# A hybrid decoder block with a product-key expert FFN: fewer dense key columns, other lists of experts gathered, and another order of the up lists

## The chip, the cores and the metric

The kernel runs on one core of one Trainium2 chip. The metric is the device time of one execution in microseconds (us), as the median of several executions. Beside the times there is one profiled execution with its trace; its times are those of single instructions on each engine.

## What is computed

One decoder layer on 256 tokens of width 2048, all in float32. An in-projection, stick-breaking attention and a chunked SSD scan, and an out-projection give h. Then comes the part that the change touches, a product-key expert layer (PEER):

```python
q = (xt @ w_query).reshape(t, 8, 2, 128)
scores = einsum('thcd,hckd->thck', q, sub_keys)          # 128 keys a half
top_s, top_i = top_k(scores, 16)
cand_i = top_i[:, :, 0, :, None] * 128 + top_i[:, :, 1, None, :]
best_s, best_pos = top_k(cand_s, 16)
expert_idx = take_along_axis(cand_i, best_pos)           # 16 of 16384 experts
gates = softmax(best_s)
act = gelu(einsum('thkd,td->thk', expert_down[expert_idx], xt))
out = einsum('thk,thkd->td', gates * act, expert_up[expert_idx])
```

So 256 tokens pick 8 x 16 experts each out of a grid of 128 x 128, and each expert has one row of 2048 numbers in the down table and one in the up table.

## The kernel before

**The front of the layer** is a stream of items (a load and the multiplications that use it), which TensorE (PE) works off in the order of the program. At its end stand 16 query items (name pq, line 253), each followed by the scores of its keys (sc, L896) and, on VectorE (DVE), by the choice of the best keys (MAX8 and FIND_INDEX8 at L900 and L901 and the reductions at L1004 to L1011).

**Dense columns.** For the last NDN columns of the key grid the product of all 128 experts with all 256 tokens is computed, whether a token picked them or not: dense(i), two items of eight float32 multiplications (dn<-xt_t,raw_dn, L253) on a load of 512 KB each, and a gelu that goes to a table in memory (zd_dram). FILL[hc] says how many of these columns stand behind query hc; all others stand behind the last query, as cover for the listing.

**The listing** (listing()) is a generator that the items advance. It transposes the picks (trT, L1115 and L1116), counts by which tokens each expert is used, ranks the experts and sorts them into NTS = 111 lists of 128 experts. yield from rest(n) lets n steps of other work pass. Before the first transposes stands rest(YT). A list's kind says who uses its experts: kinds 0 and 1 have experts that a single token of the first or second half of the tokens uses; kinds 2 and 3 have experts that two or more tokens of one half use; kinds 4 to 7 have those used in two quarters of different halves; kind 8 (C) is the rest. CAPS gives the lists of each kind. The first SPC lists of each kind hold experts from the other columns and are called sparse: their down rows are gathered by index (L1355, issued by GpSimd, POOL) and multiplied. The lists behind them hold experts of the dense columns: their values are fetched from zd_dram instead. The up rows of all lists are gathered.

**The units** multiply the down rows. unit_c(r) takes a C list: 4 items of 4 transposes (tc, L1523) and 12 multiplications of 128x256 (L1540 to L1542). unit_t(k, r) takes two lists of kinds 2 to 7: 8 items of 4 transposes (tp, L1465), a split into a high and a low part (ScalarE, ACT, at L1442 and DVE at L1443) and 6 multiplications (L1482 to L1484), and at the end two transposes back (z<-ident,zt, L1498), of which there is one pair per unit. unit_d takes a list of kind 0 or 1, a D unit: 4 items of 2 multiplications of 128x512 that give each row its token (xe or xt<-hnt,ot, L1609) and a sum over products on DVE (L1615). Beside the first units run the gates (gates(), groups g<-A,B at L1256). The units go C, then T; from the T unit with index DU = 7 on, D units are put between the items of the T units, DN of them in all.

**The up lists.** For each list 128 up rows of 2048 float32 (1.05 MB) come into a slot of a ring (5 slots during the units, 9 from begin() on). up_load splits the two halves of the row tile into a high part (ACT, L1827 or L1831) and a low part (DVE, L1828 or L1832; tile lo_up or x), and up_go multiplies both (out<-..., L1894, 128x512) with the list's weights p. split_p makes these weights: a split pair for most lists (12 multiplications for a list of one half, 24 for a C list), a one-hot matrix for sparse lists of kinds 0 and 1 (8 multiplications; the row's value is a scale of L1831 and L1832). Lists for which plain(n) holds are multiplied as they are, in float32: no split, no work on ACT or DVE for their rows, 4 multiplications.

**The order of the up lists** has an early part and three phases. The early lists are mixed with the last D units, by a time put beside each (timed); I call that the mixed stage. The early lists before are 29: two dense lists of kind 0 and the twelve lists of kind 2 (all split), then the fifteen sparse lists of kind 0, plain with a one-hot matrix scaled by the row's value (L1767). Phase 0 then has 46 lists (17 of kind 1, 12 of kind 3, 17 C), phases 1 and 2 have 18 each (14 lists of kinds 4 and 5, or 6 and 7, and NCX or NCY = 4 C lists). At the end of each phase the sums are moved (turn, L1868); the last ones are stored.

Of the kernel before, what the change touches and what calls it, by code (L numbers as in the profile page):

```python
# [14 lines left out]
OP = mybir.AluOpType  # L15
# [3 lines left out]
P = 128  # L19
T = 256  # L20
# [41 lines left out]
NCONST = K_LO + 2  # L62

NE = NK * NK
NDN = 20
NSC = NK - NDN
SPC = (15, 15, 10, 10, 6, 6, 6, 6, 20)
CAPS = (17, 17, 12, 12, 7, 7, 7, 7, 25)
LC = len(CAPS) - 1
BASE = [sum(CAPS[:k]) for k in range(LC + 1)]  # L70
# [19 lines left out]
ILAG = 2  # L90
YR = 2
YC = 2
YT = 2
GR = 1.0
KP = 0
GW = 3
# [1 line left out]
ZLAG = 4  # L98
OLAG = 7
TF = 10  # L100
XZ = 16
HU = 3
GU = 5
DU = 7
DN = 19
NPG = 4
YF = 3
HNP = 16
# [6 lines left out]
NA = 4  # L115
TD = -3
HY = 1
FILL = (0,) * 9 + (1, 0, 0, 1, 0, 0, 0)
PLP = 3
NCX = 4  # L120
NCY = 4
EV = 1
EF = (3, 1)
LP = 5
# [19 lines left out]
def tile_block(ctx: ExitStack, tc: tile.TileContext, xT, w_f, w_v, w_dt, w_o, w_q, sk, dnt, down, up,  # L144
# [55 lines left out]
    def wtile(shape, name, dt=F32):  # L200
        return wk.tile(shape, dt, tag="w", bufs=6, name=name)
# [1163 lines left out]
        pump()  # L1365

    def zh(n, w=P):
        if n < 8:
            return part["xa"][:, 3072 + P * n:3072 + P * n + w]
        if n < XZ:  # L1370
            return part["zr"][:, P * (n - 8):P * (n - 8) + w]
        n -= XZ
        if n == 0:
            gated(2)
        if n < 32:
            return held("zh", "b0")[:, P * n:P * n + w]
        return held("zh2", "b1")[:, P * (n - 32):P * (n - 32) + w]
# [6 lines left out]
    def zc(r):  # L1384
        if r < 16:
            return held("zc", "xb")[:, T * r:T * (r + 1)]
        return part["xa"][:, 2048 + T * (r - 16):2048 + T * (r - 15)]

    def zd(j):
        n = dn_of[j]  # L1390
        o = max(NTH - XZ - 32, 0) * P + sum(T if kind[i] == LC else P for i, m in dn_of.items() if m < n)
        return held("zh2", "b1")[:, o:o + (T if kind[j] == LC else P)]
# [20 lines left out]
    def dcol(k, n=1):  # L1413
        if "dsc" not in gens:
            gens["dsc"] = cp.tile([P, 8 * NDT + 128], F32, tag="gi", bufs=1, name="dsc")
        return gens["dsc"][:, NDT * k:NDT * (k + n)]
# [294 lines left out]
    for i, (_, k, r) in enumerate(ts_):  # L1711
        u_mark.append(len(items))
        u = unit_t(k, r)
        gathers += [("down", BASE[k] + r + x) for x in range(2)]
        more = 2 if len(left) > len(ts_) - i else 1
        for x in range(more if i >= DU else 0):
            n = left.pop(0)
            gathers.append(("down", d_list[n]))
            u[8 * x:8 * x + 4] = [v for p in zip(u[8 * x:8 * x + 4], dus[n]) for v in p]
        items.extend(u)  # L1720
# [3 lines left out]

    runs = [list(range(BASE[k], BASE[k] + CAPS[k])) for k in range(LC + 1)]
    ncs = (CAPS[LC] - NCX - NCY, NCX, NCY)
    order = [*runs[0][SPC[0]:], *runs[2][SPC[2]:], *runs[2][:SPC[2]], *runs[0][:SPC[0]]]
    early = len(order)
    phase = [0] * early
    for f in range(3):  # L1730
        c = runs[LC][sum(ncs[:f]):sum(ncs[:f + 1])]
        own = [runs[k] for k in range(LC) if PHASE[k] == f and k not in (0, 2)]
        if f < 2:
            order += [c[0], *mixed(*own, c[1:-1]), c[-1]]
        else:
            order += [c[0], *mixed(own[0], own[1][:-3], c[1:]), *own[1][-3:]]
        phase += [f] * (len(order) - len(phase))
# [15 lines left out]


    def plain(n):
        return n < early and kind[order[n]] == 0 and sparse[order[n]]

    def split_p(n):
        if n >= NTS or n in pw:
            return  # L1760
        j = order[n]
        k = kind[j]
        f = phase[n]
        if plain(n):
            ph = wtile([P, T], f"p{n}")[:, 0:P]
            d = d_of[j]
            TS(ph, iota[:, :, 0], dcol(7)[:, d:d + 1], dcol(2)[:, d:d + 1], op0=OP.is_equal, op1=OP.mult)  # L1767
            pw[n] = (ph, None)
            return
        if k < 2 and sparse[j]:  # L1770
            ph = wtile([P, T], f"p{n}", F32R)[:, 0:P]
            TS(ph, iota[:, :, 0], dcol(7)[:, d_of[j]:d_of[j] + 1], None, op0=OP.is_equal)
            pw[n] = (ph, None)
            return
        while j not in multiplied:
            work()
        src = zd(j) if not sparse[j] else zh(th_of[j]) if k < LC else zc(j - BASE[LC])
        if k < LC:
            w2 = wtile([P, T], f"p{n}", F32R)
            ph, pl_ = w2[:, 0:P], w2[:, P:T]  # L1780
        elif j % 2:
            ph, pl_ = [wtile([P, T], f"p{x}{n}", F32R) for x in "hl"]
        else:
            w2 = wide(f"p{n}", (P, 2 * T), F32R)
            ph, pl_ = w2[:, 0:T], w2[:, T:2 * T]
        if k < LC:
            cuts = [(slice(0, P), src[:, 0:P])]
        else:
            cuts = p_cuts(src, k, f)
        for sl, v in cuts:  # L1790
            h_, l_ = ph[:, sl], pl_[:, sl]
            if len(v.shape) == 3:
                h_, l_ = w3(h_, 64), w3(l_, 64)
            nc.scalar.activation(h_, v, AF.Copy)
            eng = nc.gpsimd if len(pw) % PLP == PLP - 1 and len(pw) > 8 else nc.vector
            eng.tensor_tensor(l_, v, h_.bitcast(F32), op=OP.subtract)
        pw[n] = (ph, pl_)
# [360 lines left out]
```

## Time and profile before

| | |
|---|---|
| Time, 3 runs | 1619.64 us median (1615.75 to 1621.01) |
| The profiled execution's own time | 1618.38 us |
| Its span, first to last instruction | 1616.5 us |
| Mean granted TensorE clock | 0.998 |
| PE busy | 1578.9 us, 98% of the span |
| DVE, ACT, POOL busy | 71%, 48%, 32% |

The span is what the views of the trace divide up; the execution's own time is 1.9 us longer. Shares of the span are means over stages that differ: a stage has to be read by itself, in a window of its own.

### The profile page before, as it was taken

How to read it: one execution, taken by the hardware profiler on the slowest of the kernel's cores; microseconds unless marked ns; L12 is line 12 of the kernel's file. 1: busy time of each engine (PE TensorE's matmuls, PEld its weight loads, DVE VectorE, ACT ScalarE, POOL GpSimd, SP SyncE). 2: the span in 40 equal slices, each digit the busy share in tenths (PEclk: the TensorE clock that was granted, in tenths of full speed). 3: DMA queues.
4: the chain of work that ended last, by engine and by line, in shares of the span. 5: the costliest groups of instructions: out<-in, count | busy, mean ns of one | idle time of the engine just before them, and what ended most of it. 6: DMA issues, size and time to landing. Idle time of an engine off the chain costs nothing.

```text
span 1616.5 us, 27319 instructions
## 1 busy us (share of the span) xinstructions
PE 1578.9 (98%) x10330; PEld 1403.3 (87%) x10331; DVE 1155.1 (71%) x2558; ACT 781.3 (48%) x1377; POOL 510.9 (32%) x495
## 2 busy tenths in 40 slices
PE   7999999999999999999999999999999999999997
PEld 7999978999888888889999999889986558887886
DVE  7776666864487988757637755878789347888896
ACT  7554557754111200525535566446555026667764
POOL 0001101111000000034415414555566455874650
PEclk9999999999999999999999999999999999999999
DMA  7555554667745534253393297788889998997983
GB/s 232 166 174 155 157 157 133 188 203 226 238 144 150 163 92 120 64 202 108 120 325 105 85 320 270 276 306 331 305 309 416 389 385 325 345 356 279 338 306 113
DMA packets 108808, 366.70 MB, mean 227 GB/s; under 512 B 12704, under 2 KB 48800, under 8 KB 82304
## 3 DMA queue, kind: packets, MB, share of 16 engines
q0 software_dynamic: 35504, 229.43, 38.3%
q1 hardware_dynamic: 70304, 134.23, 27.3%
q8 instruction: 83, 1.36, 0.3%
q10 hardware_dynamic: 2864, 1.24, 0.3%
q14 instruction: 53, 0.43, 0.1%
HBM read 337.24 MB, written 27.92 MB: 226 GB/s over the span
## 4 chain that ended last, share of the span: by engine, by line
PE 89%; DVE 5%; DMA 3%; issue 1%; ACT 1%; POOL 0%; SPq 0%; DVEq 0%; ACTq 0%; POOLq 0%
PE out L1894 21%; PE pq L253 7%; PE dn L253 7%; PE tp L1465 4%; PE g L1256 4%; PE v L735 3%; PE zc L1540 2%; PE zc L1541 2%; PE zc L1542 2%; PE z L1483 2%; PE tc L1523 2%; PE z L1484 2%; PE z L1482 2%; PE kq L312 2%; PE wo L318 2%; PE cnt L1057 2%
## 5 line engine op out<-in xcount | busy, mean ns | idle before, releaser
L1894 PE MATMUL out<-hi_up,p 128*128 128x512 f32 x716 | 193.2, 392 | 2.2 <-ACT hi_up L1827 2.2
L1894 PEld LDWEIGHTS out<-hi_up,p 128*128 128x128 f32 x716 | 134.0, 189 | 31.9 <-ACT hi_up L1827 3.9
L1443 DVE TENSOR_TENSOR t<-tp,t 128x512 fp32r<-128x512 f32 x176 | 119.7, 688 | 58.3 <-ACT t L1442 57.7
L253 PE MATMUL dn<-xt_t,raw_dn 128*128 128x256 f32 x640 | 158.6, 383 | 0.1
L1355 POOL DMA_INDIRECT raws<-in_down,idx x69 | 69.8, 1011 | 269.4 <-DVE colt L1196 161.9
L1442 ACT ACTIVATE t<-tp 128x512 fp32r<-128x512 f32 x176 | 102.8, 598 | 80.6 <-PE tp L1465 80.0
L1420 POOL DMA_INDIRECT raw_small<-g_dram,idx x111 | 119.8, 1080 | 42.5 <-issue 26.6
L253 PEld LDWEIGHTS dn<-xt_t,raw_dn 128*128 128x128 f32 x640 | 115.1, 193 | 11.6 <-issue 0.5
L253 PE MATMUL pq<-hg,raw_pq 128*128 128x256 f32 x512 | 112.9, 379 | 0.0
L253 PEld LDWEIGHTS pq<-hg,raw_pq 128*128 128x128 f32 x512 | 96.3, 190 | 12.5
L1259 ACT ACTIVATE big<-g 128x128 f32<-128x128 f32 x256 | 70.6, 436 | 74.0 <-PE g L1256 72.9
L1465 PE MATMUL tp<-ident,raws 128*128 128x128 f32 x624 | 100.4, 273 | 1.3 <-DMA raws<-in_down,idx 1.0
L1540 PE MATMUL zc<-hnl,c 128*128 128x256 f32 x320 | 96.0, 300 | 0.0
L1827 ACT ACTIVATE hi_up<-raws 128x1024 fp32r<-128x1024 f32 x74 | 77.2, 1058 | 36.7 <-PE out L1894 33.3
L1248 POOL TENSOR_TENSOR B<-B,gi 128x512 bf16<-128x512 bf16 x64 | 69.8, 1090 | 76.3 <-DVE B L1246 74.9
L1542 PE MATMUL zc<-hnl,c 128*128 128x256 f32 x320 | 89.1, 278 | 0.0
L1541 PE MATMUL zc<-hnl,c 128*128 128x256 f32 x320 | 89.1, 278 | 0.0
L1443 DVE TENSOR_TENSOR c<-tc,c 128x512 fp32r<-128x512 f32 x80 | 55.1, 690 | 39.5 <-ACT c L1442 39.1
L1827 ACT ACTIVATE hi_up<-rows_hn 128x1024 fp32r<-128x1024 f32 x66 | 69.2, 1057 | 28.2 <-PE out L1894 23.6
L1249 DVE TENSOR_TENSOR A<-O,gi 128x1024 f16<-128x1024 bf16 x64 | 49.6, 775 | 41.7 <-PE g L1256 41.6
L1894 PE MATMUL out<-lo_up,p 128*128 128x512 f32 x254 | 76.9, 395 | 1.8 <-DVE lo_up L1828 1.8
L1355 POOL DMA_INDIRECT raws<-in_up,idx x49 | 60.8, 1241 | 53.7 <-DVE lo_up L1828 17.2
(538 smaller groups left out, 4591.0 us busy)
## 6 DMA issues: line engine op xcount, KB each, us to landing
raw_dn<-in_dnt SPq DMA_DIRECT2D x40, 512.0 KB, 3.8
raw_kq<-in_w_f SPq DMA_DIRECT2D x32, 512.0 KB, 3.8
raw_wo<-in_w_o SPq DMA_DIRECT2D x32, 512.0 KB, 4.5
raw_pq<-in_w_q SPq DMA_DIRECT2D x32, 512.0 KB, 3.8
g_dram<-big SPq DMA_DIRECT2D x16, 1024.0 KB, 16.3
raw_xb<-in_w_f SPq DMA_DIRECT2D x22, 512.0 KB, 4.5
raw_v<-in_w_v SPq DMA_DIRECT2D x16, 512.0 KB, 3.6
raw_z<-in_w_f SPq DMA_DIRECT2D x16, 512.0 KB, 3.8
```

The costliest lines, as they stand in the source:

```text
L253: nc.tensor.matmul(acc, raw[:, j * P:(j + 1) * P], mv[:, k * 8 + j, :], start=(k + j == 0), stop=(k * 8 + j == ND - 1))
L1259: nc.scalar.activation(gbuf[c][:, :, o:o + G2T].rearrange("p i t -> p t i"), gp[:, :, 32 * c:32 * c + 32], AF.Copy)
L1355: g = nc.gpsimd.indirect_dma_start(out=where[what, j], out_offset=None, in_=down_rows if what == "down" else up_rows, in_offset=bass.Indir ...
L1420: nc.gpsimd.indirect_dma_start(out=dst, out_offset=None, in_=g_half if w == P else g_dram, in_offset=bass.IndirectOffsetOnAxis(ap=idx[:, 1 ...
L1442: a = nc.scalar.activation(hi, tp, AF.Copy).ins
L1443: d = nc.vector.tensor_tensor(lo, tp, hi.bitcast(F32), op=OP.subtract).ins
L1465: nc.tensor.transpose(tp[:, (2 * dd + i) * P:(2 * dd + i + 1) * P], row("down", j + i)[:, d * P:(d + 1) * P], ident)
L1540: nc.tensor.matmul(z, wh, ah[:, d, :], start=(d == 0), stop=False)
L1541: nc.tensor.matmul(z, wh, al[:, d, :], start=False, stop=False)
L1542: nc.tensor.matmul(z, wl, ah[:, d, :], start=False, stop=(d == ND - 1))
L1827: marks["act"] = nc.scalar.activation(hi, raw, AF.Copy).ins
L1894: nc.tensor.matmul(oa[tt][2 * hf + c], w[:, k * P:(k + 1) * P], mv[:, c * 512:(c + 1) * 512], start=(i == starts[f, tt, hf] and mv is hi a ...
```

## The change

Four dense columns fewer (NDN 20 to 16), all of them now behind the last query (FILL). Two C lists more are sparse (SPC 20 to 22), so two lists fewer are fetched from zd_dram. YT goes from 2 to 9. Twenty-four D units instead of 19 stand in the T units, spread evenly: nine of the fifteen T units take two and six take one, where before the first four took two. The early lists are now 8 sparse lists of kind 2, and these are plain: the up rows are multiplied in float32 with the float32 weights (zh). The 17 lists of kind 0 and the 4 other lists of kind 2 go to phase 0, mixed with those of kinds 1 and 3, and are split there; the lists of kind 0 get the one-hot form of L1772. NCX and NCY go from 4 to 2, so phase 0 has 21 C lists and 71 lists in all, and phases 1 and 2 have 16 each. XZ and zh place the weights elsewhere.

```diff
--- before.py
+++ after.py
@@ -62,9 +62,9 @@
 NCONST = K_LO + 2
 
 NE = NK * NK
-NDN = 20
+NDN = 16
 NSC = NK - NDN
-SPC = (15, 15, 10, 10, 6, 6, 6, 6, 20)
+SPC = (15, 15, 10, 10, 6, 6, 6, 6, 22)
 CAPS = (17, 17, 12, 12, 7, 7, 7, 7, 25)
 LC = len(CAPS) - 1
 BASE = [sum(CAPS[:k]) for k in range(LC + 1)]
@@ -90,7 +90,7 @@
 ILAG = 2
 YR = 2
 YC = 2
-YT = 2
+YT = 9
 GR = 1.0
 KP = 0
 GW = 3
@@ -98,11 +98,12 @@
 ZLAG = 4
 OLAG = 7
 TF = 10
-XZ = 16
+XZ = 12
 HU = 3
 GU = 5
 DU = 7
-DN = 19
+DN = 24
+NE0 = 8
 NPG = 4
 YF = 3
 HNP = 16
@@ -115,10 +116,10 @@
 NA = 4
 TD = -3
 HY = 1
-FILL = (0,) * 9 + (1, 0, 0, 1, 0, 0, 0)
+FILL = (0,) * 16
 PLP = 3
-NCX = 4
-NCY = 4
+NCX = 2
+NCY = 2
 EV = 1
 EF = (3, 1)
 LP = 5
@@ -1365,10 +1366,10 @@
         pump()
 
     def zh(n, w=P):
-        if n < 8:
-            return part["xa"][:, 3072 + P * n:3072 + P * n + w]
+        if n < 4:
+            return part["xa"][:, 3584 + P * n:3584 + P * n + w]
         if n < XZ:
-            return part["zr"][:, P * (n - 8):P * (n - 8) + w]
+            return part["zr"][:, P * (n - 4):P * (n - 4) + w]
         n -= XZ
         if n == 0:
             gated(2)
@@ -1712,7 +1713,7 @@
         u_mark.append(len(items))
         u = unit_t(k, r)
         gathers += [("down", BASE[k] + r + x) for x in range(2)]
-        more = 2 if len(left) > len(ts_) - i else 1
+        more = 2 if (i - DU) * (DN - len(ts_) + DU) % (len(ts_) - DU) < DN - len(ts_) + DU else 1
         for x in range(more if i >= DU else 0):
             n = left.pop(0)
             gathers.append(("down", d_list[n]))
@@ -1724,12 +1725,12 @@
 
     runs = [list(range(BASE[k], BASE[k] + CAPS[k])) for k in range(LC + 1)]
     ncs = (CAPS[LC] - NCX - NCY, NCX, NCY)
-    order = [*runs[0][SPC[0]:], *runs[2][SPC[2]:], *runs[2][:SPC[2]], *runs[0][:SPC[0]]]
+    order = runs[2][:NE0]
     early = len(order)
     phase = [0] * early
     for f in range(3):
         c = runs[LC][sum(ncs[:f]):sum(ncs[:f + 1])]
-        own = [runs[k] for k in range(LC) if PHASE[k] == f and k not in (0, 2)]
+        own = [[j for j in runs[k] if j not in order] for k in range(LC) if PHASE[k] == f]
         if f < 2:
             order += [c[0], *mixed(*own, c[1:-1]), c[-1]]
         else:
@@ -1753,7 +1754,7 @@
 
 
     def plain(n):
-        return n < early and kind[order[n]] == 0 and sparse[order[n]]
+        return n < early
 
     def split_p(n):
         if n >= NTS or n in pw:
@@ -1761,12 +1762,6 @@
         j = order[n]
         k = kind[j]
         f = phase[n]
-        if plain(n):
-            ph = wtile([P, T], f"p{n}")[:, 0:P]
-            d = d_of[j]
-            TS(ph, iota[:, :, 0], dcol(7)[:, d:d + 1], dcol(2)[:, d:d + 1], op0=OP.is_equal, op1=OP.mult)
-            pw[n] = (ph, None)
-            return
         if k < 2 and sparse[j]:
             ph = wtile([P, T], f"p{n}", F32R)[:, 0:P]
             TS(ph, iota[:, :, 0], dcol(7)[:, d_of[j]:d_of[j] + 1], None, op0=OP.is_equal)
@@ -1775,6 +1770,9 @@
         while j not in multiplied:
             work()
         src = zd(j) if not sparse[j] else zh(th_of[j]) if k < LC else zc(j - BASE[LC])
+        if plain(n):
+            pw[n] = (src[:, 0:P], None)
+            return
         if k < LC:
             w2 = wtile([P, T], f"p{n}", F32R)
             ph, pl_ = w2[:, 0:P], w2[:, P:T]
```

In what follows the first rows are PE's around the scores of the last query, the start of the listing. sc are the scores, dn a dense column (x8: eight multiplications in a row), trT the listing's first transposes. Before:

```order
L896 MATMUL sc_5507<-big_72,qs_5380 128x128 x2
L253 MATMUL dn_5524<-xt_t,raw_dn_0_5397 128x256 x8
L253 MATMUL dn_5524<-xt_t,raw_dn_1_5431 128x256 x8
L253 MATMUL dn_5648<-xt_t,raw_dn_0_5471 128x256 x6
L1115 MATMUL trT<-ident,big_69 128x128
L253 MATMUL dn_5648<-xt_t,raw_dn_0_5471 128x256 x2
L1116 MATMUL trT<-ident,big_69 128x128
L1115 MATMUL trT<-ident,big_69 128x128
L1116 MATMUL trT<-ident,big_69 128x128
```

Twenty-two multiplications of dense columns stand between the last scores and the first trT. After, at the same place of PE:

```order
L897 MATMUL sc_5459<-big_72,qs_5322 128x128 x2
L254 MATMUL dn_5476<-xt_t,raw_dn_0_5349 128x256 x8
L254 MATMUL dn_5476<-xt_t,raw_dn_1_5383 128x256 x8
L254 MATMUL dn_5547<-xt_t,raw_dn_0_5423 128x256 x8
L254 MATMUL dn_5547<-xt_t,raw_dn_1_5441 128x256 x4
L1116 MATMUL trT<-ident,big_69 128x128
L254 MATMUL dn_5547<-xt_t,raw_dn_1_5441 128x256 x3
L1117 MATMUL trT<-ident,big_69 128x128
L1116 MATMUL trT<-ident,big_69 128x128
L1117 MATMUL trT<-ident,big_69 128x128
L254 MATMUL dn_5547<-xt_t,raw_dn_1_5441 128x256
```

Twenty-eight stand there now, and no dense column stands ahead of the last query any more.

The next rows are PE's in the mixed stage. out00 to out03 are the sums of the first half of the tokens, hi_up and lo_up a list's split rows, p its weights, xe a D unit's products. Before, the first nine of the twelve multiplications of one list of kind 2:

```order
L1894 MATMUL out00_13294<-hi_up3_0_13411,p3_13334 128x512
L1894 MATMUL out01_13295<-hi_up3_0_13411,p3_13334 128x512
L1894 MATMUL out00_13294<-hi_up3_0_13411,p3_13334 128x512
L1894 MATMUL out01_13295<-hi_up3_0_13411,p3_13334 128x512
L1894 MATMUL out02_13296<-hi_up3_1_13430,p3_13334 128x512
L1894 MATMUL out03_13297<-hi_up3_1_13430,p3_13334 128x512
L1894 MATMUL out00_13294<-lo_up3_0_13412,p3_13334 128x512
L1894 MATMUL out01_13295<-lo_up3_0_13412,p3_13334 128x512
L1894 MATMUL out02_13296<-hi_up3_1_13430,p3_13334 128x512
```

Each of them reads a tile that ACT or DVE has made of the gathered row. After, plain lists between D units (raws, xa are ring slots with rows as they were gathered; xa and zh also hold weights):

```order
L1610 MATMUL xe1_13471<-hnt0_10510,ot24_13101 128x512
L1610 MATMUL xe1_13471<-hnt1_10680,ot24_13101 128x512
L1892 MATMUL out00_13474<-raws_6894,xa2_7208 128x512
L1892 MATMUL out01_13475<-raws_6894,xa2_7208 128x512
L1892 MATMUL out02_13476<-raws_6894,xa2_7208 128x512
L1892 MATMUL out03_13477<-raws_6894,xa2_7208 128x512
L1892 MATMUL out00_13474<-xa2_7208,zh2_13246 128x512
L1892 MATMUL out01_13475<-xa2_7208,zh2_13246 128x512
L1892 MATMUL out02_13476<-xa2_7208,zh2_13246 128x512
L1892 MATMUL out03_13477<-xa2_7208,zh2_13246 128x512
L1610 MATMUL xe2_13472<-hnt0_10510,ot24_13101 128x512
```

A list of kind 2 was 12 multiplications on four split tiles; it is now 4 multiplications on the gathered rows, with no tile of a split in it.

The last rows are PE's in phase 0. out1 are the sums of the second half of the tokens, ph and pl a C list's split weights. Before, a one-hot list (30) with the C list 31 behind it:

```order
L1894 MATMUL out10_13984<-hi_up30_0_14002,p30_13963 128x512
L1894 MATMUL out11_13985<-hi_up30_0_14002,p30_13963 128x512
L1894 MATMUL out10_13984<-lo_up30_0_14003,p30_13963 128x512
L1894 MATMUL out11_13985<-lo_up30_0_14003,p30_13963 128x512
L1894 MATMUL out12_13986<-hi_up30_1_14021,p30_13963 128x512
L1894 MATMUL out13_13987<-hi_up30_1_14021,p30_13963 128x512
L1894 MATMUL out12_13986<-lo_up30_1_14022,p30_13963 128x512
L1894 MATMUL out13_13987<-lo_up30_1_14022,p30_13963 128x512
L1894 MATMUL out00_13294<-hi_up31_0_14031,ph31_13975 128x512
```

One list of 8 multiplications stands there, then a list of 24. After, where list 38 of kind 0 ends and list 39 of kind 1 follows it:

```order
L1892 MATMUL out02_13476<-hi_up38_1_14491,p38_14424 128x512
L1892 MATMUL out03_13477<-hi_up38_1_14491,p38_14424 128x512
L1892 MATMUL out02_13476<-x3_13479,p38_14424 128x512
L1892 MATMUL out03_13477<-x3_13479,p38_14424 128x512
L1892 MATMUL out10_13654<-hi_up39_0_14499,p39_14445 128x512
L1892 MATMUL out11_13655<-hi_up39_0_14499,p39_14445 128x512
L1892 MATMUL out10_13654<-lo_up39_0_14500,p39_14445 128x512
L1892 MATMUL out11_13655<-lo_up39_0_14500,p39_14445 128x512
L1892 MATMUL out12_13656<-hi_up39_1_14512,p39_14445 128x512
L1892 MATMUL out13_13657<-hi_up39_1_14512,p39_14445 128x512
L1892 MATMUL out12_13656<-lo_up39_1_14513,p39_14445 128x512
L1892 MATMUL out13_13657<-lo_up39_1_14513,p39_14445 128x512
```

One-hot lists of the first half now stand next to one-hot lists of the second half, in 15 such pairs, so that two lists of 8 multiplications come before the next longer list.

## Rows read from the trace of the kernel before

**Rows 1.** The page, busy time: us, share of the span, instructions.

```profile
PE 1578.9 (98%) x10330; PEld 1403.3 (87%) x10331; DVE 1155.1 (71%) x2558; ACT 781.3 (48%) x1377; POOL 510.9 (32%) x495
```

**Rows 2.** Windows of the last 400 us: busy us (instructions) of each engine, clock, DMA share, GB/s.

```profile
1196.00:1256.00 60.00, 55.26 (x224) 40.60 (x223) 53.98 (x118) 31.43 (x49) 39.28 (x34) 0.97 0.98 396
1256.00:1318.00 62.00, 61.56 (x165) 30.47 (x163) 22.04 (x77) 3.21 (x11) 31.17 (x34) 1.00 0.97 378
1318.00:1485.00 167.00, 165.46 (x758) 137.03 (x759) 133.16 (x188) 108.49 (x133) 114.49 (x92) 1.00 0.93 344
1485.00:1580.00 95.00, 94.58 (x415) 77.17 (x414) 83.21 (x99) 67.69 (x98) 53.07 (x41) 1.00 0.86 310
```

**Rows 3.** Timeline of PE at a dense column: start us, us, records.

```profile
477.57 7.07 PE L253 MATMUL dn<-xt_t,raw_dn 128*128 128x256 f32 x32
484.48 0.61 PE L896 MATMUL sc<-big,qs 128*128 128x128 f32 x4
```

**Rows 4.** The chain that ended last, in a stretch of phase 0.

```profile
1353.83 103.55 PE out L1894 x456
```

**Rows 5.** Timeline of PE at the first unsplit up lists.

```profile
1256.26 3.59 PE L1894 MATMUL out<-xa,p 128*128 128x512 f32 x8
1259.69 1.02 PE L1894 MATMUL out<-raws,p 128*128 128x512 f32 x2
```

**Rows 6.** Timeline of PE in the units of C lists.

```profile
844.39 0.60 PE L1523 MATMUL tc<-ident,raws 128*128 128x128 f32 x4
...
846.25 1.12 PE L1256 MATMUL g<-A,B 128*128 128x128 f16 x8
847.19 0.62 PE L1523 MATMUL tc<-ident,raws 128*128 128x128 f32 x4
```

**Rows 7.** Windows, L1894 alone (up multiplications), first part of the mixed stage.

```profile
1196.00:1256.20 60.20, 43.84 (x168) 32.01 (x169) 0.97 0.98 396
```

**Rows 8.** Windows, L1609 alone (D multiplications), the same stretch.

```profile
1196.00:1256.20 60.20, 15.28 (x48) 8.06 (x48) 0.97 0.98 396
```

**Rows 9.** Windows around one wait of PE in the mixed stage.

```profile
1243.00:1248.00 5.00, 2.04 (x7) 1.35 (x8) 4.86 (x10) 1.74 (x4) 2.95 (x3) 0.95 1.01 408
1248.00:1251.00 3.00, 3.00 (x10) 2.27 (x8) 2.15 (x7) 1.88 (x2) 2.05 (x3) 0.52 1.01 412
```

**Rows 10.** Timeline of PE, L1498 alone: each T unit's transposes back.

```profile
1011.32 0.38 PE L1498 MATMUL z<-ident,zt 128*128 128x128 f32 x2
...
1024.38 0.38 PE L1498 MATMUL z<-ident,zt 128*128 128x128 f32 x2
...
1066.70 0.38 PE L1498 MATMUL z<-ident,zt 128*128 128x128 f32 x2
...
1083.59 0.38 PE L1498 MATMUL z<-ident,zt 128*128 128x128 f32 x2
```

**Rows 11.** Timeline of PE, first transposes of the listing.

```profile
561.93 0.33 PE L1115 MATMUL trT<-ident,big 128*128 128x128 f32 x1 [2.06 <-DVE big L1006]
...
563.87 0.33 PE L1116 MATMUL trT<-ident,big 128*128 128x128 f32 x1 [0.74 <-DVE big L1011]
```

**Rows 12.** Timeline of DVE, waits for the scores of two queries.

```profile
506.74 0.30 DVE L900 MAX8 slot<-sc 128x8 f32<-128x128 f32 x1 [3.57 <-PE sc L896]
...
514.09 0.30 DVE L900 MAX8 slot<-sc 128x8 f32<-128x128 f32 x1 [4.49 <-PE sc L896]
```

**Rows 13.** Timeline, the first row gather and the first C transposes.

```profile
689.91 1.03 POOL L1355 DMA_INDIRECT raws<-in_down,idx  x1 [161.86 <-DVE colt L1196]
...
725.93 1.06 PE L1523 MATMUL tc<-ident,raws 128*128 128x128 f32 x8
```

**Rows 14.** The view of DMA issues: xcount, us from issue to landing.

```profile
raws<-in_down,idx POOLq DMA_INDIRECT x69, 7.8
```

**Rows 15.** Groups by form, DVE in phase 0: busy us, mean ns, idle before.

```profile
L1828 DVE TENSOR_TENSOR lo_up<-raws,hi_up 128x1024 fp32r<-128x1024 f32 x24 | 29.3, 1236 | 5.1 <-ACT hi_up L1827 5.0
...
L1832 DVE SCALAR_TENSOR_TENSOR lo_up<-rows_hn,dsc,hi_up 128x1024 fp32r<-128x1024 f32 x12 | 15.5, 1294 | 7.8 <-ACT hi_up L1831 7.8
```

## The prediction

> **What bounds the kernel now.** I read the page first: TensorE (PE) is busy in 98% of the span, VectorE (DVE) in 71% [rows 1]. So the sum of PE's work is nearly the time, and an edit is worth what it takes off PE, less what PE then waits. Next I cut the end into stages by windows: the reader is to see PE busy for 165.5 of 167 us in phase 0, for 94.6 of 95 in most of phases 1 and 2 and for 61.6 of 62 in the plain part of the mixed stage, but only for 55.3 of 60 in its split part, where DVE is busy for 54.0 [rows 2]. That is the one place where DVE sets the pace. DVE's share is 80% in phase 0 and 88% in phases 1 and 2: it is next. The DMA engines are at 0.98, 0.97, 0.93 and 0.86 of those stages, so row transfers come close behind. Then I took PE's prices from the timeline and the chain, since durations of single multiplications overlap: distances between starts are what counts.
>
> **Prices.** A split multiplication of 128x512 takes 103.55 / 456 = 0.227 us [rows 4]: 1.82 for a one-hot list (8), 2.72 for a split list of one half (12), 5.45 for a C list (24). A plain list takes 1259.69 − 1256.26 = 3.43 us [rows 5]. A dense column takes 484.48 − 477.57 = 6.91 us [rows 3].
>
> **The change part by part,** against the span of 1616.5 us:
>
> 1. Four dense columns fewer: 4 x 6.91 = −27.6 us. Their loads of 1 MB each go too; PE did not wait for them. FILL only moves two of the other columns from between the queries to behind them.
> 2. Two C units more: an item takes 847.19 − 844.39 = 2.80 us, of which the gate group takes 847.19 − 846.25 = 0.94, so 1.86 by itself [rows 6]; 8 items make +14.9 us. The gate groups aren't more than before. Two gathers of 1.05 MB come with the units; two fetches from the table of dense values go.
> 3. Fifteen lists of kind 0 go from plain to one-hot split: 15 x (1.82 − 3.43) = −24.2 us. What they now cost elsewhere is 30 passes of ACT and DVE, paid for below.
> 4. Eight lists of kind 2 go from split to plain: 8 x (3.43 − 2.72) = +5.7 us. Their 16 passes of about 1.24 us on DVE [rows 15] go, and their weights need no split.
> 5. Five D units go from the mixed stage into the T units. On PE this is 8 x 0.227 = 1.82 each at either place: 0.
> 6. The mixed stage stops waiting. In its split part 168 up multiplications [rows 7] and 48 of D units [rows 8] would take 216 x 0.227 = 49.1 us; it took 60.2. So 11.1 us are waits for DVE, what the clock loses behind them, and some small transposes. After, no list in this stage is split: six D units (10.9 us of PE) and eight plain lists (27.4) need from DVE little more than the D units' sums. The plain part of before is this mix: PE was busy for 61.6 of 62 us, DVE for 22.0 [rows 2]. I take −9, between 0 (the waits move with the D units) and −11.
> 7. The T units take the D units. Distances between the transposes back show it: a unit with two D units took 1024.38 − 1011.32 = 13.06 us, which leaves 13.06 − 3.64 = 9.4 without them; one stretch shortly behind the four doubles, with one D unit, took 1083.59 − 1066.70 = 16.89 where 11.3 was due [rows 10]. So four doubles in a row are not always free, as rows come late after them. Nine doubles spread over fifteen units give the gathers a break after each one or two. I take 0, between −8 (the excess goes) and +26 (below).
> 8. The listing's start. PE had waited 2.06 + 0.74 = 2.80 us for the picks at trT [rows 11]. Without the two filled columns PE arrives 2 x 6.91 − 6 x 0.216 = 12.5 us sooner (six more dense multiplications of 0.216 = 6.91 / 32 each stand before trT). The picks come sooner too: DVE had waited 3.57 and 4.49 us for scores that stood behind a filled column [rows 12]. Between 0 and 12.5 − 8.1 = +4.4; I take +2, since DVE had further small waits there.
> 9. The listing's end. From the first row gather to the first C transposes were 36.0 us [rows 13], filled by dense columns and gates. Two columns less as cover are 13.8, and some 8 us of gate groups go behind the C items instead, which leaves 14 or so; a gather lands after 7.8 [rows 14]. So the rows are still in time; +2, between 0 and +6 if four gathers queue on POOL.
> 10. New waits in the phases. Phase 0 keeps its 133 us of DVE and gets 15 one-hot lists (two passes of 1.29 [rows 15] and a one-hot each, some 2.9), six split lists and four C lists (two passes of 1.24 and the weights' split, some 2.9 as an estimate), 72 us in all, while PE gets 15 x 1.82 + 6 x 2.72 + 4 x 5.45 = 65. That makes 205 of 232 us, 88%. Phases 1 and 2 lose 4 C lists, the ones in which PE is long and DVE short: for a stretch like the 95 us shown, PE 94.6 − 3.2 x 5.45 = 77, DVE 83.2 − 3.2 x 2.9 = 74, 96%. What is late there is lo_up, and PE's next list behind it. I take +7, between 0 and +31.
>
> Sum: −27.6 + 14.9 − 24.2 + 5.7 − 9 + 0 + 2 + 2 + 7 = −29.2. The profiled execution took 1618.4, so 1589 for one like it; it lay 1.3 below the median of the runs, so **1590 us**.
>
> **A rule beside the row.** Over 60 us this core moved 396 GB/s and over 62 us 378, almost all of it gathered rows [rows 2]. The Trainium skill (DMA: Bandwidth & Descriptors, Specifications) gives a limit of about 358 GB/s for what a core gets from memory. By that limit the rows below would need 360 us where the sum has 348, the new waits would be +12 and the time an estimated 1596. The trace does not agree: two stages ran above it.
>
> **The rivals.**
> - *Row transfers become the bound.* From 1196 to 1580 the windows moved 134.1 MB (each rate by its length) in 384 us. Five D gathers go ahead of it: 128.9 MB, and by the terms above the stretch would last 384 − 9.1 − 24.2 + 5.7 − 9 = 347 us, 371 GB/s. If the engines give no more than the 344 of phase 0, it lasts 375: +28 in place of +7, 1611 us. For it: the DMA share of 0.93 at 344. Against it: 378 and 396 in the stages where the ring asked for more; PE waited for no row there.
> - *Slower: short lists in pairs.* In phase 0, 15 times two one-hot lists now stand together: PE needs 3.64 us, DVE 5.72. If each pair makes PE wait the 2.1 us and the clock then falls as behind the wait in [rows 9] (granted 0.52, the level of 1.2 GHz, for 3 us with PE busy throughout: 1.4 us lost), a pair costs 3.5, 15 pairs 53: 1590 − 7 + 53 = 1636. It decides from 12 of 15 pairs on (1590 − 7 + 42 = 1625, 0.3% slower). Against it: a C list stands behind most pairs, and leaves DVE 5.45 − 2.9 = 2.5 us to catch up; three tiles of hi_up and of low parts each let it work ahead.
> - *The T units lose.* If each double takes the 16.89 that the worst unit took, 9 x (16.89 − 13.1) = 34, less the excess of about 8 that is there now: +26, 1616, no change.
> - *The mixed stage goes on waiting,* for D rows that come late rather than for splits: the 9 stay, 1599.
> - *No new waits anywhere:* −7 − 8 from terms 7 and 10 and −2 from term 9, 1573 to 1576.
>
> **How the numbers follow.** Chances: the forecast, within 8 us, 0.50; no new waits 0.15; transfers 0.14; the mixed stage waits on 0.07; T units 0.06; pairs 0.08. A measurement of this kernel can tell about 0.3%, 5 us, from no change. Faster by more than that are the forecast, no new waits, the waiting mixed stage, four fifths of the transfers and a few of the T units and the pairs that fall short of 12: 0.84. Slower are the pairs, 0.08. The same are the rest, 0.08. The range leaves out the pairs, half of the T units and the lower half of "no new waits": 1576 to 1613.
>
> **What would show it.** Right: no dn between the queries and 16 x 32 records of dn; a window over the mixed stage of about 39 us with PE above 95%; one-hot lists of kind 0 at 1.82 us; 1416 up multiplications from the end of the mixed stage in some 340 us. Wrong: PE waiting for lo_up or x (DVE) in phases 1 and 2 by more than 15 us, a granted clock below 0.97 in a slice of phase 0, waits for rows (DMA) at L1465, L1523 or in hi_up's ACT pass, or two trT waits of more than 8 us. The prediction falls if PE's busy time drops by the 31 us of terms 1 to 4 and the span does not.

## The result and the profile after

The changed kernel took 1596.76 us (median of 4 runs, 1595.53 to 1599.74), the kernel before beside it 1618.12: a ratio of 0.9872, with a 95% interval of 0.9855 to 0.989, so 18 to 23 us faster. 1590 had been forecast, in a range of 1576 to 1613. The profiled execution took 1595.53 us, its span 1593.7 against 1616.5.

The page of the changed kernel, busy time (compare [rows 1]): PE's busy time fell by 23.0 us, as much as the span (22.8). It is still 98% of it, so no other engine became the bound as a whole. Terms 1 to 4 were to take 31 us off PE; that the busy time shows only 23 has one reason that recurs below: a multiplication that starts late often leaves no idle time in the records, so lost time can count as busy.

```profile
PE 1555.9 (98%) x10298; PEld 1386.2 (87%) x10299; DVE 1176.1 (74%) x2569; ACT 794.1 (50%) x1379; POOL 527.1 (33%) x492
```

To see where the time went I cut both executions at the same instructions: the end of the last scores, the first transpose of a T unit, the first D unit of the mixed stage, the first split multiplication of phase 0, the last up multiplication. Lengths in us, worked out from the starts in the timeline of PE:

```
stage                                   before   after    change   the prediction's terms
up to the last scores                    550.4   533.9    -16.5    -13.8 (two columns moved away)
listing, dense columns, gates, C units   378.2   385.8     +7.6    +5.1 (1, 2, 8, 9, less the -13.8)
T units                                  267.5   278.8    +11.3    +9.1 (5, 7)
mixed stage                              122.9    41.5    -81.4    -80.2 (lists, 5, 6)
phases 0 to 2                            289.4   346.0    +56.6    +50.6 (lists, 10)
```

2.7 us of the first line had come before the first query (404.1 against 401.4), in a part that the change does not touch: scatter. The mixed stage came out as forecast. The phases are the main difference, 6 us.

Windows of the changed kernel, the mixed stage, phase 0, and phases 1 and 2 (start and end, length, busy us and instructions of PE, PEld (PE's weight loads), DVE, ACT and POOL, then clock, DMA share, GB/s; compare [rows 2]): the mixed stage has PE busy for 40.9 of 41.5 us and DVE for 22.3, so its wait for splits is gone. Phase 0 has DVE at 82% and 361 GB/s, phases 1 and 2 have DVE at 92%.

```profile
1198.50:1240.00 41.50, 40.92 (x124) 21.08 (x123) 22.30 (x85) 5.25 (x15) 24.52 (x26) 1.00 0.97 383
1240.00:1486.50 246.50, 241.04 (x1058) 192.25 (x1057) 202.88 (x267) 166.90 (x199) 170.52 (x128) 0.99 0.94 361
1486.50:1586.00 99.50, 98.09 (x426) 78.85 (x424) 91.95 (x102) 70.81 (x91) 48.72 (x34) 1.00 0.75 269
```

Due in phase 0 are 984 multiplications of 0.227 and 7 us of small ones that add h (L1843), some 231 us; it took 246.5 to the last move of its sums, where before phase 0 took 168.4 for 165. So some 12 us of new waits lie in phase 0, though PE's records show it busy for 241.0. Phases 1 and 2 took 99.5 for 98: almost none lie there.

The start of the listing, timeline of PE and two windows (in brackets the idle time ahead of a record and what ended it; compare [rows 11]): the wait at trT doubled to 5.52, and behind it the clock was granted at 0.60 on average over four microseconds with PE busy throughout, the lower of its two levels (1.2 GHz) for most of them. The three dense multiplications behind it (6 records, 1.3 us at full rate) took 2.6, until 554.31.

```profile
551.48 0.48 PE L1116 MATMUL trT<-ident,big 128*128 128x128 f32 x1 [5.52 <-DVE big L1007]
551.75 2.77 PE L254 MATMUL dn<-xt_t,raw_dn 128*128 128x256 f32 x6
554.31 0.42 PE L1117 MATMUL trT<-ident,big 128*128 128x128 f32 x1
```

```profile
548.00:552.00 4.00, 0.52 (x2) 0.52 (x3) 4.00 (x5) 0.00 (x0) 0.00 (x0) 0.55 0.00 0
552.00:556.00 4.00, 4.00 (x14) 3.25 (x14) 2.01 (x7) 0.29 (x1) 0.00 (x0) 0.60 0.02 4
```

The mixed stage, timeline of PE: a plain list and a D unit (8 multiplications, L1610) take 1224.19 − 1218.77 = 5.42 us together, which with 3.43 for the list [rows 5] leaves 2.0 for the D unit, not 8 x 0.227 = 1.82.

```profile
1218.77 3.60 PE L1892 MATMUL out<-rows_hn,zh 128*128 128x512 f32 x8
1221.80 2.55 PE L1610 MATMUL xe<-hnt,ot 128*128 128x512 f32 x8
1224.19 3.60 PE L1892 MATMUL out<-rows_hn,zh 128*128 128x512 f32 x8
```

One of phase 0's waits, timeline of all engines: DVE stands at a weight (zh, L1678) whose gates raw_small, a gather, are 2.48 us late; the low part lo_up (L1826) stands behind it on DVE's queue, and PE waits 1.27 us for that. ACT waits 2.38 us for rows at the same time. This is the largest such place, not a typical one; the sums are with the runs halflo and halflo2 below.

```profile
1284.52 0.36 DVE L1678 TENSOR_TENSOR zh<-zh,raw_small 128x64 f32<-128x64 f32 x2 [2.48 <-DMA raw_small<-g_dram,idx]
...
1284.79 1.22 DVE L1826 TENSOR_TENSOR lo_up<-rows_hn,hi_up 128x1024 fp32r<-128x1024 f32 x1
...
1286.07 1.21 PE L1892 MATMUL out<-lo_up,ph 128*128 128x512 f32 x4 [1.27 <-DVE lo_up L1826]
1286.10 1.15 ACT L1829 ACTIVATE hi_up<-rows_hn,dsc 128x1024 fp32r<-128x1024 f32 x1 [2.38 <-DMA raws<-in_up,idx]
```

### The profile page after: what moved, and what is told of

The parts are those of the page before. It is cut to its first block, busy times and chain, and to the rows that moved or that the text cites. A ratio compares the mean times of both kernels' runs of the same rounds, so it can differ in the third digit from the quotient of the medians.

```text
span 1593.7 us, 27287 instructions
## 1 busy us (share of the span) xinstructions
PE 1555.9 (98%) x10298; PEld 1386.2 (87%) x10299; DVE 1176.1 (74%) x2569; ACT 794.1 (50%) x1379; POOL 527.1 (33%) x492
## 5 line engine op out<-in xcount | busy, mean ns | idle before, releaser
L1356 POOL DMA_INDIRECT raws<-in_down,idx x77 | 76.9, 999 | 293.7 <-DVE idx L1192 163.1
L1421 POOL DMA_INDIRECT raw_small<-g_dram,idx x111 | 115.9, 1044 | 58.4 <-issue 23.2
L254 PE MATMUL dn<-xt_t,raw_dn 128*128 128x256 f32 x512 | 131.8, 387 | 0.1
L1541 PE MATMUL zc<-hnl,c 128*128 128x256 f32 x352 | 105.5, 300 | 0.0
L254 PEld LDWEIGHTS dn<-xt_t,raw_dn 128*128 128x128 f32 x512 | 92.0, 196 | 8.7 <-issue 0.5
L1543 PE MATMUL zc<-hnl,c 128*128 128x256 f32 x352 | 98.0, 278 | 0.0
L1542 PE MATMUL zc<-hnl,c 128*128 128x256 f32 x352 | 98.0, 278 | 0.0
L1444 DVE TENSOR_TENSOR c<-tc,c 128x512 fp32r<-128x512 f32 x88 | 60.8, 690 | 48.3 <-ACT c L1443 48.1
L1825 ACT ACTIVATE hi_up<-rows_hn 128x1024 fp32r<-128x1024 f32 x70 | 73.5, 1059 | 31.8 <-PE out L1892 28.9
L1892 PE MATMUL out<-lo_up,p 128*128 128x512 f32 x274 | 84.6, 400 | 2.6 <-DVE lo_up L1830 1.6
L1356 POOL DMA_INDIRECT raws<-in_up,idx x48 | 68.4, 1425 | 44.7 <-DVE lo_up L1826 9.3
L1356 POOL DMA_INDIRECT rows_hn<-in_up,idx x50 | 70.1, 1401 | 38.2 <-DVE lo_up L1826 8.9
```

The source lines that it names most:

```text
L254: nc.tensor.matmul(acc, raw[:, j * P:(j + 1) * P], mv[:, k * 8 + j, :], start=(k + j == 0), stop=(k * 8 + j == ND - 1))
L1356: g = nc.gpsimd.indirect_dma_start(out=where[what, j], out_offset=None, in_=down_rows if what == "down" else up_rows, in_offset=bass.Indir ...
L1421: nc.gpsimd.indirect_dma_start(out=dst, out_offset=None, in_=g_half if w == P else g_dram, in_offset=bass.IndirectOffsetOnAxis(ap=idx[:, 1 ...
L1444: d = nc.vector.tensor_tensor(lo, tp, hi.bitcast(F32), op=OP.subtract).ins
L1541: nc.tensor.matmul(z, wh, ah[:, d, :], start=(d == 0), stop=False)
L1542: nc.tensor.matmul(z, wh, al[:, d, :], start=False, stop=False)
```

## The experiments

The runs came in three groups, each on one chip beside the kernel before. In the second group every kernel was slower by some 2%, the kernel before too (1654.02); in apart, the T units take 40 us longer than in the changed kernel, which has the same ones. Ratios of that group are not set against the others; its windows of phase 0 are read with that reservation.

```
run        us        before    ratio [95% interval]
after      1596.76   1618.12   0.9872 [0.9855, 0.989]
dense16    1614.81   1619.05   0.9975 [0.9965, 0.9985]
lists20    1612.02   1619.05   0.9957 [0.9941, 0.9974]
fill       1604.71   1619.05   0.9917 [0.9901, 0.9934]
dn19       1591.88   1619.05   0.9838 [0.9822, 0.9854]
dn15       1622.55   1654.02   0.9809 [0.9778, 0.984]
halflo     1639.77   1654.02   0.9911 [0.9884, 0.9939]
halfrow    1637.47   1654.02   0.9897 [0.9856, 0.9939]
apart      1646.27   1654.02   0.9959 [0.994, 0.9978]
yt16       1597.36   1618.66   0.9869 [0.9854, 0.9885]
dn19yt16   1590.19   1618.66   0.9826 [0.9813, 0.9839]
dn15yt16   1593.07   1618.66   0.9841 [0.9827, 0.9854]
halflo2    1592.49   1618.66   0.9839 [0.9824, 0.9854]
```

**dense16: the dense columns alone.** The kernel before with these edits, and zh() as in the changed kernel:

```diff
-NDN = 20
+NDN = 16
-SPC = (15, 15, 10, 10, 6, 6, 6, 6, 20)
+SPC = (15, 15, 10, 10, 6, 6, 6, 6, 22)
-XZ = 16
+XZ = 12
```

> The kernel before with 16 dense columns and 22 gathered C lists alone (and the places of the weights that go with them); the order of the up lists, the D units, the columns behind queries 9 and 12 and the 2 steps ahead of the first transposes stay as before. My theory: PE's work is the time, so minus 27.6 for four columns, plus 14.9 for two C units, plus 0 to 2 for cover: 12 us faster than before, 1606. Rival: the columns were cover for the listing on VectorE, and what they leave is waited: at most 5 us faster, 1613.

It was 4.2 us faster, the rival's number. Timeline of PE and windows where the listing ends, in this run: PE runs out of dense columns and waits for gates (0.74) and for the first gathered rows (2.22); then the clock is granted at 0.50 for 4.5 us with PE busy throughout. In the kernel before these places had no wait at all.

```profile
693.83 1.10 PE L1256 MATMUL g<-A,B 128*128 128x128 f16 x8 [0.74 <-DVE A L1249]
697.15 1.75 PE L1523 MATMUL tc<-ident,raws 128*128 128x128 f32 x7 [2.22 <-DMA raws<-in_down,idx]
```

```profile
693.00:698.00 5.00, 2.03 (x13) 1.76 (x13) 5.00 (x6) 1.42 (x5) 3.97 (x4) 0.82 0.93 350
698.00:702.50 4.50, 4.50 (x21) 3.75 (x20) 2.93 (x6) 1.19 (x2) 3.44 (x3) 0.50 0.23 91
```

From the last scores to the first T unit it takes 375.7 us where the kernel before takes 378.2: of the 12.7 us less work, 10 are given back there.

**lists20: the other part alone.** The changed kernel with NDN, SPC, XZ, zh(), FILL and YT as before.

> The other part alone: the changed kernel with 20 dense columns, 20 gathered C lists, the columns behind queries 9 and 12 and 2 steps as before; only the D units in the T units, the plain early lists and the phases are changed. My theory: minus 24.2 plus 5.7 for the lists, minus 9 for the mixed stage, plus about 2 in the T units and 13 of new waits in the phases: 12 us faster than before, 1606. Rival: the phases gain from the shorter rest of the kernel and lose by themselves, so that the lists alone give 4 us at most.

7.0 us faster (interval 4 to 10): between the two theories, nearer to the rival. The two parts alone give 4.2 + 7.0 = 11 us; together, without the moved columns, 14 (the next run).

**fill: two columns between the queries again, and YT as before.**

```diff
-YT = 9
-FILL = (0,) * 16
+YT = 2
+FILL = (0,) * 9 + (1, 0, 0, 1, 0, 0, 0)
```

> The changed kernel with dense columns behind queries 9 and 12 again and 2 steps ahead of the first transposes, as before. My theory: these two columns only moved the wait at the transposes; it goes back from 5.5 us to about 3, and the clock does not fall there, so the time is 0 to 4 us less than that of the changed kernel. Rival: they held VectorE's choice of keys back by 8 us, which then comes back as later picks: 3 us or more slower than the changed kernel.

My theory fell: it was slower than the changed kernel, 0.9917 against 0.9872, intervals that do not touch, about 7 us. The waits at trT did go back (2.07 and 0.74), but where the listing ends PE again waits for rows and gates, as in dense16. These are the waits of PE from 680 to 930 us (total, times, longest), in fill and then in the changed kernel:

```profile
PE g L1257 <- DVE A L1250: 2.2, 2, 1.4
PE tc L1524 <- DMA raws<-in_down,idx: 2.0, 1, 2.0
```

```profile
PE tc L1524 <- DVE c L1444: 0.3, 1, 0.3
```

So the moved columns pay at the end of the listing, as cover. How much is less sure than the times say: from the first query to the first T unit, the part that this edit touches, the traces show 520.4 us in fill and 518.3 in the changed kernel, 2 of the 7 us. Where the other 5 lie no trace shows.

**yt16: more cover at trT.**

```diff
-YT = 9
+YT = 16
```

> The changed kernel with 16 steps ahead of the first transposes instead of 9, which puts 40 dense multiplications there instead of 28 and takes 5 us of cover from the listing's end. My theory: the wait of 5.5 us at the transposes goes and with it the 3 us that the clock then loses, and the end had some 4 us of cover to spare: 4 to 8 us faster than the changed kernel (0.9872 of before), so 0.982 to 0.985. Rival: the listing on VectorE is the bound, and what PE does not wait for at the transposes it waits for at the end: within 2 us of the changed kernel, 0.986 to 0.9885.

0.9869 against 0.9872: the rival. The waits at trT fell from 5.52 to 1.98 us, as the timeline of PE in this run shows, and the clock does not fall behind them, some 5 us in all. Part of it came back as the rival had it: where the listing ends PE now waits 1.8 us for gates, a wait that the changed kernel does not have, and the clock is at its lower level for 3.4 us behind it. The first T unit started 3 us earlier (counted from the first query); the times do not show it.

```profile
554.18 0.33 PE L1116 MATMUL trT<-ident,big 128*128 128x128 f32 x1 [0.38 <-DVE big L1007]
556.10 0.33 PE L1117 MATMUL trT<-ident,big 128*128 128x128 f32 x1 [1.60 <-DVE big L1012]
```

```profile
PE g L1257 <- DVE A L1250: 1.8, 1, 1.8
```

**dn19, dn15, dn19yt16, dn15yt16: fewer D units in the T units.** DN = 19 or 15 in place of 24 in the changed kernel, without and with YT = 16.

> The changed kernel with 19 D units in the T units, 4 doubles spread evenly, and 11 in the mixed stage beside the 8 plain lists. My theory: a D unit costs PE 1.8 us at either place, so 9 us move from the T units to the mixed stage and the time stays within 3 us of the changed kernel. Rival: with 24 the T units are held up by late rows or VectorE, and 19 are 4 us or more faster; or the mixed stage cannot take 11 D units among 8 lists, and 19 are 4 us or more slower.

> The changed kernel with 15 D units in the T units, one in each and no doubles, and 15 in the mixed stage. My theory by now: a D unit costs PE 2.4 us at either place, but doubles in T units lose 1 to 3 us each, and a longer mixed stage lets rows and gates run ahead of phase 0, so 15 are 2 to 6 us faster than 19, which gave 1592: 1586 to 1590. Rival: 19 was already free of this, and 15 D units among 8 lists wait for VectorE or rows: same as 19 or slower, 1592 to 1598.

> 19 D units in the T units, spread evenly, and 16 steps ahead of the transposes: both at once in the changed kernel. If the two gains are independent, as they lie in different stages: 0.9838 of before for the first, and 4 to 8 us for the second, so 0.979 to 0.981. If either was the scatter of its chip: 0.984 to 0.987.

> The same with 15 D units in the T units and 15 in the mixed stage. If doubles in the T units cost beyond the D units' own work also with four of them: 2 to 5 us faster than the kernel with 19. If four doubles are free and the mixed stage then waits for the D units' one-hot matrices or rows: the same or up to 5 us slower.

19 is faster than 24 in both pairs: 0.9838 against 0.9872, and 0.9826 against 0.9869. dn19yt16 is the fastest kernel here by its median, 28 us below the kernel before; its interval overlaps that of dn19. 15 is not faster still: 1593.07 against 1590.19 on the same chip (dn15 came from the other chip and says nothing on this). The stages (us, cut as above):

```
                T units   mixed stage   both    phases 0 to 2
before           267.5       122.9      390.4       289.4
changed (24)     278.8        41.5      320.3       346.0
dn19 (19)        262.0        55.0      317.0       341.7
yt16 (24)        279.0        41.4      320.4       345.4
dn19yt16 (19)    262.7        56.7      319.4       341.6
dn15yt16 (15)    251.1        65.3      316.3       343.7
```

With the same 19 D units the spread over the T units saves 4.8 us against the kernel before. Five more cost 16.3 there, 3.3 each, though a D unit is 2.0 by itself. But this is not where the gain lies: taken out of the mixed stage they make it 15.3 shorter, 3.1 each, so both stages together differ by 1.0 us (3.3 in the other pair). The larger part, 3.8 us (4.3 in the other pair), lies in the phases, of which more below. With 15 both stages together are 3.1 us shorter again, but the phases are 2.1 longer; from the first query to the first T unit, where no D unit stands, that run also took 518.1 us against 515.3, so these two runs say little on which of 19 and 15 is better.

Single stretches between the transposes back say little: in the changed kernel one of 15.1 us (from 1146.73) holds 20 of the T units' multiplications of L1483 and one D unit, the next, of 11.6 us, 12 and two D units. A unit has 16.

**halflo and halflo2, halfrow, apart: what phase 0 waits for.** In halflo and halflo2 VectorE's low parts are half as wide, and TensorE uses that half twice, so a part of the computation is left out (one of the three edited lines):

```diff
-            marks["dve"] = nc.vector.tensor_tensor(lo, raw, hi.bitcast(F32), op=OP.subtract).ins
+            marks["dve"] = nc.vector.tensor_tensor(lo[:, 0:512], raw[:, 0:512], hi[:, 0:512].bitcast(F32), op=OP.subtract).ins
```

In halfrow each up gather is out=where[what, j][:, 0:1024] from a view of the table with rows of 4 KB, used for both halves of the output; in apart phase 0 is mixed(long, short), with the lists of kinds 0 and 1 in short.

> The changed kernel in which VectorE makes the low part of each split up row for half of the columns only, and TensorE uses that half twice; a part of the computation is left out, the same number of multiplications stays. If the 15 us that phase 0 loses are VectorE's passes: they fall to 5 us or less and the time to about 1586. If they are rows and gates that arrive late: not more than 4 us change, 1593 to 1598.

> The changed kernel with up rows of 4 KB gathered instead of 8 KB, used for both halves of the output; a part of the computation is left out, all engines' instructions stay. If the 15 us that phase 0 loses are row transfers at the limit of the DMA engines: they go, and the time falls to about 1584. If they are VectorE's passes: not more than 4 us change, 1593 to 1598.

> The changed kernel with the lists of phase 0 in another order: each one-hot list of kinds 0 and 1 stands between two longer lists, so no two of them are neighbours. If pairs of one-hot lists cause phase 0's waits, as the rival of the prediction has it: 5 to 12 us faster, 1585 to 1592. If rows or gates come late, or VectorE is late as a whole: within 3 us of the changed kernel.

> Again the changed kernel in which VectorE makes the low part of each split up row for half of the columns only (a part of the computation is left out), beside a kernel with whole low parts on the same chip. If VectorE's passes are what phase 0 loses: from the first split multiplication to the last of phase 0 it takes 10 to 13 us less than the kernel with 16 steps does there, and the whole about 12 us less than the changed kernel, 0.980 of before. If it is rows and gates: within 4 us of it.

Against yt16 on the same chip, halflo2 has phase 0 in 239.9 us instead of 246.0; these are the windows of yt16 and then of halflo2:

```profile
1239.80:1485.80 246.00, 240.67 (x1058) 190.70 (x1057) 202.37 (x267) 167.19 (x198) 172.53 (x128) 1.00 0.95 363
```

```profile
1241.10:1481.00 239.90, 235.28 (x1058) 192.41 (x1057) 132.20 (x267) 166.01 (x199) 129.74 (x128) 1.00 0.97 372
```

DVE's work fell by 70 us, phase 0 by 6: about half of the 12 us of new waits, below the 10 to 13 that I expected if they were DVE's passes, above nothing. Two more readings of the traces say what phase 0 waits for. First, where a multiplication starts more than 0.227 us behind the one ahead of it, the excess can be put to the tile that it reads (sums over phase 0 in us, worked out from the starts of PE; the small multiplications of L1843 left out):

```
             phase 0   ahead of low parts (DVE)   ahead of high parts (ACT)
before         168.4              1.1                        1.7
changed        246.5             11.5                        3.6
yt16           246.0             11.2                        3.5
dn19yt16       242.1              6.5                        4.4
halflo2        239.9              5.2                        3.3
```

So 10 of the 12 us are waits for low parts; 8 of them stand at low parts of one-hot lists (0.2 before). Second, dn19yt16 differs from yt16 by the D units alone, and in its phase 0 the gates come in time: DVE's waits for them there (total, times, longest) are these in yt16, and the last line in dn19yt16.

```profile
DVE zh L1678 <- DMA raw_small<-g_dram,idx: 6.2, 6, 2.5
DVE zh L1666 <- DMA raw_small<-zd_dram,idx: 1.8, 1, 1.8
```

```profile
DVE zh L1671 <- DMA raw_small<-zd_dram,idx: 1.1, 1, 1.1
```

Phase 0 is 4 us shorter with that, and 5 us fewer are lost ahead of low parts; that the longer mixed stage ahead gives the gates this time is argued, not shown. In halflo2 the gates are as late as ever (11.1 us), and 6 us fewer are lost. So neither theory alone holds: some 4 of the 12 us go when the gates come in time (dn19 and the changed kernel show the same, 242.3 and 246.5), some 6 when DVE's passes for the low parts are halved.

halflo on the other chip has 236.8, halfrow 238.6 and apart 242.3; dn15, the only kernel there with whole passes and rows in the changed order, has 243.8. Against that, narrower rows take off nearly as much as narrower low parts, and one-hot lists apart from each other little. But dn15 has the longer mixed stage, and no run of the changed kernel itself stands beside them on that chip, so the shares of rows and pairs stay open.

## Why the prediction came out

The direction, the size and the mechanism (PE's work is the time) held: 21 us of 29. Point by point:

- **Terms 1 and 2, −27.6 and +14.9:** PE's records bear them out (128 records of dn fewer, 32 of each line of zc more), but the term had costed the moved columns at nothing. Four columns fewer without the moved ones give 4 us, not 13 (dense16): the columns are the listing's cover, and where they run out PE waits and its clock falls. That the changed kernel does not lose this is due to FILL and YT together, about 7 us by the times of fill, 2 by its trace. The sum came out because terms 1, 8 and 9 were worked out with the columns already moved.
- **Term 8, +2:** mis-sized. The wait rose by 2.7, and the clock behind it took some 2 more (PE worked at the lower level for some 3.7 us). One slip: a dense multiplication is two records, 0.43 us and not 0.216, so the six more cost 2.6.
- **Term 9, +2:** the waits there are 0.3.
- **Terms 3 and 4, −24.2 and +5.7:** within the mixed stage's −81.4 against −80.2.
- **Terms 5 and 7, 0:** a D unit is 2.0 us of PE and not 1.82; I had priced it by the up multiplications. The spread took away 5 us of the excess, as hoped, and the five more D units gave it back: 11.3 us in the T units, where five times 2.0 were due. The size of that excess was misread, though: the stretch of 16.89 us in [rows 10] holds 20 of the T units' multiplications of L1482, that of 13.06 holds 14, where a unit has 16. By those counts some 13.6 us were due in the first and not 11.3, and the worst unit, on which the rival of the T units rests, was less bad than it looked.
- **Term 6, −9:** held; the mixed stage took 41.5 us, where six D units at 2.0 and eight plain lists at 3.43 make 39.4.
- **Term 10, +7:** the step that failed. About 13, and in phase 0 instead of phases 1 and 2, where DVE is at 92% and PE loses 1 us. That low parts would be late was right; the share of DVE did not say where. They are late at the one-hot lists and behind late gates, and phases 1 and 2 have no one-hot lists.
- **The rivals:** transfers as the bound (1611) did not come, but late gates are part of term 10; phase 0 ran at 361 GB/s. By the limit that the Trainium skill gives (DMA: Bandwidth & Descriptors, Specifications: about 358 GB/s) the estimate was 1596, which is what was measured. The mixed stage's 383 and phase 0's 361 GB/s still lie above that limit, so the agreement is not its doing. Short lists in pairs did not cost 3.5 us a pair, but one-hot lists are the place of 8 of the 12 us. One of the prediction's signs of being wrong, a granted clock below 0.97 in a slice of phase 0, came once (0.957 in a fortieth of the span): behind waits for the tiles of one-hot lists the clock was at its lower level for 3.4 us with PE busy throughout, 1.7 us lost.

```profile
1323.30:1326.60 3.30, 3.30 (x8) 2.62 (x9) 0.12 (x1) 2.23 (x2) 2.82 (x4) 0.50 0.94 355
```

- **The rival of the T units:** they lost 6 us to the nine doubles beyond the D units' own work (16.3 for five, 10 due), not 26, and the mixed stage was 15.3 us shorter for these five.

## What to carry to other kernels

Work that fills an engine's time while a chain on another engine runs is worth its length only as long as it is longer than the chain: cost its removal at the place where the chain ends, with the clock that falls behind the wait. Count a moved piece of work at both of its places, and look at what follows: five D units cost 3.3 us each in the T units and 3.1 in the mixed stage, though 2.0 by themselves, and what moving them was worth lay mostly in the stage behind. Where DVE at 92% costs PE 1 us and at 82% some 10, ask which tile the late multiplication reads and what stands ahead of that tile in its engine's queue, not how busy the engine is.

## What was not expected of the hardware

On the second group's chip the same kinds of programs took 2% longer, in apart most of it in the T units: 318.9 us in apart against 278.8 in the changed kernel, which has the same T units, while from the last scores to the first T unit they agree (386.1 and 385.8). Timeline of ACT in apart: it waits 3.70 us for something that the trace knows only as remote; waits on remote add up to some 15 us on ACT in apart's T units. All four traces of that chip have such waits, and none of the ten others has one.

```profile
1098.08 0.38 ACT L1494 ACTIVATE zt<-z 128x256 f32<-128x256 f32 x1 [3.70 <-remote]
```

What that is, no run here shows.
